# Attention scores in PSUM tiles of two banks, in a hybrid decoder layer on one Trainium2 core

## The chip, the core and the metric

The program runs on one NeuronCore of a Trainium2 chip. TensorE (PE in the profile) multiplies, VectorE (DVE), ScalarE (ACT) and GpSimd (POOL) do the rest, and SyncE (SP) issues the transfers. TensorE writes into PSUM, which has eight banks here; one bank holds 512 float32 numbers in each of 128 partitions. The metric is the device time of one execution in microseconds (us). The time before is 1449.49 us, the median of three runs that lie between 1445.99 and 1454.82 us.

## What is computed

One decoder layer on a sequence of 1024 tokens: a modulation from a conditioning vector, one input projection, two groups of attention heads side by side, an output projection, and a gated feed-forward layer with a short convolution. Only the attention matters here:

```
group A (8 heads, 96 numbers in q and k): scores of all keys up to the query, softmax, times v
group B (8 heads, 64 numbers in q and k): the same, over three dilated windows that are combined
                                          by their softmax denominators
mix = concat(A, B) @ w_o
```

The kernel does group B as one dense attention too: a mask that is added to the scores holds minus the logarithm of how many of the three windows take a key (and a large number where none does), so both groups run through the same code with two different masks. Every product is made of three: an operand is split into a rounded part `hi` and a rest `lo`, and hi x hi, hi x lo and lo x hi are added up in PSUM.

## The kernel before

**The attention stage.** Eight couples of heads are worked through, four of group B (called dilated here) and four of group A (called MLA), in the order 0, 4, 1, 5, 2, 6, 3, 7, so that a dilated couple and an MLA couple alternate (L690 to L709). For each couple there are two halves of the queries, `hf` 0 and 1, of four blocks of 128 queries each. Block `qi` sees `w = 128 * (qi + 1)` keys, so the rows of the first half are 128, 256, 384 and 512 wide and those of the second 640, 768, 896 and 1024.

**Scores** (`scores`, L624). A row of scores needs three matmuls per 512 columns at most. A row of the first half goes into one PSUM bank, tile `s`; a row of the second half is cut into two equal parts of 320, 384, 448 and 512 columns, each with a bank of its own. VectorE then adds the mask, writes the sum to SBUF (`pt`) and keeps the smallest number of each row, in one instruction per bank (L642, shown as CUSTOM_DVE, with a short DVE_READ_ACCUMULATOR2 behind it); the second part of a wide row starts from the smallest number of the first part (its operand `st`). ScalarE takes the exponential with its row sum (L646), GpSimd turns the sum into its inverse (L647) and scales the row (L648). The buffers of `pt` are two for each block number, one per head (`P_BUFS`).

**The two heads of a couple on TensorE.** The heads of a dilated couple have 64 numbers each and lie in partitions 0 to 63 and 64 to 127 of the same tiles `q2` and `k2`; their matmuls use 64 of the 128 rows of TensorE (64\*128 in the rows of the trace). The heads of an MLA couple have 96 numbers and tiles of their own (96\*128). For a dilated couple the source puts the matmuls of both heads next to each other (`together`).

**Weighted values** (`weighted_values`, L662). The scaled rows are turned by TensorE, four blocks of 128 x 128 into one bank (tile `x`, L671); ScalarE writes the rounded part `pT_hi` (L677), VectorE the rest `pT_lo` (L678), which reads the same bank and sets it free; two matmuls per tile, one with `hi` and one with `lo`, add to the output in tile `o` (L682). A half of a couple has 6 such `x` tiles for `hf` 0 and 14 for `hf` 1. The half that is worked through is the one before (`pending`), so that weighted values of one half stand beside the scores of the next. The turned q and k of the next couple (`transposed`, L529 to L533) use banks of the same pool `x`: L529 on TensorE, L531 on ScalarE, L532 on VectorE.

**PSUM in this stage** (L614): 3 banks for `x`, 2 for `o`, 3 for `s`.

**What sets the order.** The instructions are recorded in the order of the source, and a scheduler then puts them in order for each engine by a simulated timeline: an instruction can move past others of its engine where its operands and buffers are free earlier. The couple's matmuls that stand next to each other in the source need not do so in the program. Each engine then works through its own list in that order.

Of the kernel before, what the change touches and what calls it, by code (L numbers as in the profile page):

```python
# [8 lines left out]
F32 = mybir.dt.float32  # L9
# [3 lines left out]
AF = mybir.ActivationFunctionType  # L13
ALU = mybir.AluOpType
# [4 lines left out]
P = 128  # L19
S = 1024  # L20
# [11 lines left out]
P_BUFS = 2  # L32
# [9 lines left out]
def hybrid_layer(ctx, tc, x, c, positions, w_ada, b_ada, g_mix_norm, w_in, g_q_lat, w_q_b, g_kv_lat, w_kv_b,  # L42
# [3 lines left out]
    V, G, A, T = nc.vector, nc.gpsimd, nc.scalar, nc.tensor  # L46
    x, c, out = x[0], c, out[0]
# [10 lines left out]
    def psum_phase(**tags):  # L58
        psum.close()
        pools.clear()  # L60
        for tag, n in tags.items():
            pools[tag] = psum.enter_context(
                tc.tile_pool(name="ps_" + tag, bufs=n, space=PSUM, reuse_waits="tile"))
# [3 lines left out]
    def bank(tag="bank"):  # L67
        return pools[tag].tile([P, 512], F32, tag=tag, name=tag)

    def wide():  # L70
        return pools["wide"].tile([P, 1024], F32, tag="wide", name="wide")
# [41 lines left out]
    negone = cp.tile([P, 1], F32, name="negone")  # L113
# [150 lines left out]
    def proj_weights(c0, n):  # L264
        raw = raw_tile(KD, n)
        nc.sync.dma_start(raw, w_in[:, c0:c0 + n].rearrange("(k p) n -> p k n", p=P))
        return split_weights(raw, KD, n)
# [5 lines left out]
    def proj_mm(w, t, n):  # L273
        ps = bank("p")
        for k in range(KD):
            proj_step(ps, w, t, n, k)
        return ps
# [59 lines left out]
    ap = phA.enter_context(tc.tile_pool(name="phAw", bufs=1, reuse_waits="tile"))  # L337
# [103 lines left out]
    w = proj_weights(C_KV, 288)  # L441
    for t in range(NT):
# [3 lines left out]
        ps = proj_mm(w, t, 288)  # L446
# [9 lines left out]
        b = ap.tile([P, 1, ROPE], F32, tag="peb", name="peb", bufs=2)  # L456
# [7 lines left out]
    for u in range(2):  # L464
# [6 lines left out]
        w = proj_weights(C_VD + u * 256, 256)  # L471
        for t in range(NT):
            ps = proj_mm(w, t, 256)
            o = ap.tile([P, 256], F32, tag="vo", name="vo", bufs=6)
# [16 lines left out]
    for hf in range(2):  # L491
        cs = slice(hf * 512, hf * 512 + 512)
        for src, hi, lo, n, g0 in ((q_lat, ql_hi, ql_lo, 4, G0_QL), (kv_lat, kl_hi, kl_lo, 2, G0_KV)):
            for f in range(n):
                ps = bank("x")
# [57 lines left out]
    for u in range(2):  # L553
        raw = raw_tile(4, 384)
        nc.sync.dma_start(raw, w_q_b[:, u * 384:(u + 1) * 384].rearrange("(k p) n -> p k n", p=P))
        w = split_weights(raw, 4, 384)
        for t in range(NT):
            ts_ = slice(t * P, (t + 1) * P)
            ps = bank("p")
# [12 lines left out]
            o = mp.tile(b3, F32, tag="ro", name="rom", bufs=4)  # L572
# [6 lines left out]
            b = mp.tile(bp, F32, tag="rb", name="rbm", bufs=3)  # L579
# [4 lines left out]
    for u in range(2):  # L584
        raw = raw_tile(2, 512)
        nc.sync.dma_start(raw, w_kv_b[:, u * 512:(u + 1) * 512].rearrange("(k p) n -> p k n", p=P))
        w = split_weights(raw, 2, 512)
        for t in range(NT):
            ts_ = slice(t * P, (t + 1) * P)
            ps = bank("p")  # L590
            for k in range(2):
# [11 lines left out]
            o = mp.tile([P, 4, MW], F32, tag="ro", name="rok", bufs=4)  # L603
            V.tensor_tensor(o[:, :, 0:NOPE], p3[:, :, 0:NOPE], r[:, :, None].to_broadcast(b3), op=ALU.mult)
            G.tensor_scalar(o[:, :, NOPE:MW], k_pe[:, t:t + 1, :].to_broadcast([P, 4, ROPE]), 1.0, 0.0,
                            op0=ALU.mult, op1=ALU.add)
# [4 lines left out]
    more_weight_buffers(None, 0)  # L611


    psum_phase(x=3, o=2, s=3)  # L614
    phM = ExitStack()
    mxp = phM.enter_context(tc.tile_pool(name="mixbuf", bufs=1, reuse_waits="tile"))
    mix = mxp.tile([P, 8, S], F32, name="mix")
# [2 lines left out]
    ap = phB.enter_context(tc.tile_pool(name="phB", bufs=1, reuse_waits="tile"))  # L620
    GROUPS = ([((0, 0),), ((1, 1), (3, 3)), ((2, 2),)],
              [((0, 0),), ((1, 0),), ((2, 0),), ((3, 0),), ((4, 0),), ((5, 1), (7, 3)), ((6, 2),)])

    def scores(hf, heads, mask, together):  # L624
        prs = [[] for _ in heads]
        for group in ([heads] if together else [[h] for h in heads]):
            for i in range(4):
                qi = 4 * hf + i
                w = P * (qi + 1)
                qs_ = slice(qi * P, (qi + 1) * P)  # L630
                cuts = [(0, w)] if w <= 512 else [(0, w // 2), (w // 2, w)]
                pts = [ap.tile([P, w], F32, tag=f"pt{qi}", name=f"pt{qi}", bufs=P_BUFS) for _ in group]
                sts = [ap.tile([P, 4], F32, tag="st", name="st", bufs=16) for _ in group]
                for n, (a, b) in enumerate(cuts):
                    pss = [bank("s") for _ in group]
                    for m in range(len(group[0])):
                        for ps, terms in zip(pss, group):
                            q_, k_ = terms[m]
                            T.matmul(ps[:, 0:b - a], lhsT=q_[:, qs_], rhs=k_[:, a:b], start=(m == 0),  # L639
                                     stop=(m == len(terms) - 1))  # L640
                    for ps, pt, st in zip(pss, pts, sts):
                        V.tensor_tensor_reduce(pt[:, a:b], ps[:, 0:b - a], mask[:, S - w + a:S - w + b], 1.0,  # L642
                                               3.0e38 if n == 0 else st[:, n - 1:n], ALU.add, ALU.min, st[:, n:n + 1])
                m = len(cuts) - 1
                for terms, pt, st in zip(group, pts, sts):
                    A.activation(pt, pt, AF.Exp, bias=st[:, m:m + 1], scale=-1.0, accum_out=st[:, 2:3])  # L646
                    G.tensor_tensor(st[:, 3:4], st[:, 2:3], negone, op=ALU.pow)  # L647
                    G.tensor_scalar(pt, pt, st[:, 3:4], 1.0, op0=ALU.mult, op1=ALU.mult)  # L648
                    prs[[h is terms for h in heads].index(True)].append(pt)
        return prs  # L650

    evac = [0]
# [40 lines left out]
    for n, pr in enumerate(ORDER):  # L693
        mask = masks[:, 1 if pr < 4 else 0, :]
# [89 lines left out]
    for hf in range(2):  # L784
# [4 lines left out]
        for cch in range(4):  # L789
# [6 lines left out]
            w = split_weights(raw, KD, 256)  # L796
            pss = []
            for i in range(4):
                ps = bank()
# [234 lines left out]
    for hf in range(2):  # L1034
        pss = {(i, u): bank("d") for i in range(4) for u in range(2)}
# [13 lines left out]
        for ff in range(NFF):  # L1049
            w, m = down_parts(ff), m_parts(ff, hf)  # L1050
# [6 lines left out]
        for i in range(4):  # L1057
            t = 4 * hf + i
            for u in range(2):
# [3 lines left out]
                o = fp.tile([P, 512], F32, tag="s", name="o", bufs=4)  # L1063
# [43 lines left out]
```

## Time and profile before

| | |
|---|---|
| median of three runs | 1449.49 us |
| the profiled execution: device time | 1452.97 us |
| its span, first to last instruction | 1451.0 us |
| granted TensorE clock, mean | 0.979 |
| TensorE busy | 1376.4 us, 95% |
| VectorE busy | 972.6 us, 67% |
| GpSimd busy | 795.5 us, 55% |
| ScalarE busy | 727.4 us, 50% |
| the attention stage, in the span | 352 to 652 us |

The profiled execution is one run; its device time is the span and 1.97 us around it, and it lies 3.5 us above the median. In the stage's 300 us TensorE is busy for 285.2 us, VectorE for 247.5, ScalarE for 237.7. A matmul's busy time includes the end of its way through the array, though, so two that follow each other overlap; what a matmul costs is read from start to start. "Idle before" in a row is the time in which the engine had nothing under way, with what ended it. Columns are times from the span's start.

### The profile page before, as it was taken

What the parts mean: (1) busy time and instruction counts of PE and PEld (TensorE: products, weight loads), DVE (VectorE), ACT (ScalarE), POOL (GpSimd) and SP (SyncE); (2) the same over time, 40 slices, a digit from 0 to 9 for tenths busy, and PEclk for the clock granted to TensorE, in tenths of its full rate; (3) what the DMA queues carried; (4) which work ended last, traced back from release to release, by engine and by line L of the source; (5) the groups of instructions that cost most, each with busy time, mean ns of one, the idle gap of its engine ahead of it and who ended that gap; (6) DMA issues with size and microseconds to landing.
All of it is one profiled execution on the core that took longest, in us unless ns stands there. A gap on an engine that the chain in (4) does not pass through costs nothing.

```text
span 1451.0 us, 22006 instructions
## 1 busy us (share of the span) xinstructions
PE 1376.4 (95%) x7837; PEld 1178.1 (81%) x7837; DVE 972.6 (67%) x1834; ACT 727.4 (50%) x1409; POOL 795.5 (55%) x780
## 2 busy tenths in 40 slices
PE   5889999998999998989989799999999999999998
PEld 3789999996778786779978688888888887888887
DVE  3667888687878888875655767777777765226213
ACT  3524322376778887864444644455455454322320
POOL 3355656367766667534624275656655554555552
PEclk9999999999999999999999899999999999999999
DMA  9643354546121114003535122222222238445431
GB/s 320 197 149 120 125 184 158 112 152 212 31 59 45 59 45 116 2 17 124 195 114 177 59 97 76 88 88 71 75 87 88 87 113 307 162 144 191 160 113 58
DMA packets 140197, 173.31 MB, mean 119 GB/s; under 512 B 7986, under 2 KB 118968, under 8 KB 139960
## 3 DMA queue, kind: packets, MB, share of 16 engines
q1 hardware_dynamic: 140088, 171.92, 36.5%
q8 instruction: 61, 1.00, 0.3%
q14 instruction: 48, 0.39, 0.1%
HBM read 135.19 MB, written 36.70 MB: 118 GB/s over the span
## 4 chain that ended last, share of the span: by engine, by line
PE 63%; DVE 5%; DMA 4%; POOL 3%; ACT 3%; issue 3%; SPq 0%; DVEq 0%; POOLq 0%; ACTq 0%
PE d L1045 16%; PE X L877 16%; PE Z L877 8%; PE Y L877 5%; PE o L682 5%; PE s L639 4%; PE x L671 4%; DMA raw<-in_w_o_dram 2%; POOL w_lo L98 2%; PE p L103 1%; DVE pt L642 1%; PE p L104 1%; PE p L105 1%; ACT pt L646 1%; PE bank L105 1%
## 5 line engine op out<-in xcount | busy, mean ns | idle before, releaser
L1045 PE MATMUL d<-wd,m 128*128 128x512 f32 x1056 | 240.0, 389 | 3.2 <-ACT m L1028 3.0
L1045 PEld LDWEIGHTS d<-wd,m 128*128 128x128 f32 x1056 | 198.0, 188 | 45.1 <-ACT m L1028 3.4
L830 POOL TENSOR_TENSOR wa<-sum,wa 128x512 fp32r<-128x512 f32 x80 | 135.1, 1692 | 119.0 <-ACT wa L829 118.1
L1021 POOL TENSOR_TENSOR wd<-raw,wd 128x512 fp32r<-128x512 f32 x88 | 132.5, 1528 | 112.0 <-ACT wd L1018 96.3
L877 PE MATMUL X<-T,wa 128*128 128x512 f32 x720 | 172.2, 392 | 8.6 <-ACT wa L829 8.6
L103 PE MATMUL p<-w_hi,h_hi 128*128 128x256 f32 (+1 forms) x576 | 165.2, 288 | 3.2 <-ACT xn L362 3.2
L877 PEld LDWEIGHTS X<-T,wa 128*128 128x128 f32 x720 | 136.3, 190 | 37.6 <-ACT wa L829 9.0
L98 POOL TENSOR_TENSOR w_lo<-raw,w_hi 128x512 fp32r<-128x512 f32 (+3 forms) x74 | 109.8, 1514 | 97.8 <-ACT w_hi L92 97.8
L104 PE MATMUL p<-w_lo,h_hi 128*128 128x256 f32 (+1 forms) x576 | 163.4, 285 | 0.0
L105 PE MATMUL p<-w_hi,h_lo 128*128 128x256 f32 (+1 forms) x576 | 161.1, 286 | 1.0 <-DVE h_lo L262 1.0
L830 POOL TENSOR_TENSOR wa<-raw,wa 128x512 fp32r<-128x512 f32 x68 | 100.8, 1488 | 85.9 <-ACT wa L829 85.4
L1029 DVE TENSOR_TENSOR m<-m_raw,m 128x512 fp32r<-128x512 f32 x44 | 54.4, 1242 | 123.9 <-ACT m L1028 123.9
L1018 ACT ACTIVATE wd<-raw 128x1024 fp32r<-128x1024 f32 x44 | 46.6, 1059 | 142.6 <-PE d L1045 117.5
L647 POOL TENSOR_TENSOR st<-st,negone 128x1 f32<-128x1 f32 x128 | 69.9, 553 | 83.7 <-ACT pt L646 72.7
L103 PEld LDWEIGHTS p<-w_hi,h_hi 128*128 128x128 f32 x576 | 111.1, 193 | 3.6 <-ACT xn L362 3.4
L104 PEld LDWEIGHTS p<-w_lo,h_hi 128*128 128x128 f32 x576 | 111.4, 193 | 0.1
L678 DVE TENSOR_TENSOR pT_lo<-x,pT_hi 128x512 fp32r<-128x512 f32 (+1 forms) x160 | 98.0, 633 | 19.6 <-ACT pT_hi L677 18.5
L105 PEld LDWEIGHTS p<-w_hi,h_lo 128*128 128x128 f32 x576 | 109.0, 192 | 1.6 <-DVE h_lo L262 1.6
L677 ACT ACTIVATE pT_hi<-x 128x512 fp32r<-128x512 f32 (+1 forms) x160 | 86.0, 553 | 46.0 <-PE x L671 39.5
L929 DVE SCALAR_TENSOR_TENSOR y<-c,ccols,y 128x1023 f32<-128x1023 f32 x44 | 60.5, 1376 | 62.3 <-ACT y L928 61.5
L646 ACT ACTIVATE pt<-pt,st 128x256 f32<-128x256 f32 (+7 forms) x128 | 98.5, 772 | 6.3 <-DVE st L642 6.1
L648 POOL TENSOR_SCALAR pt<-pt,st 128x256 f32<-128x256 f32 (+7 forms) x128 | 97.6, 768 | 6.6
(265 smaller groups left out, 3385.4 us busy)
## 6 DMA issues: line engine op xcount, KB each, us to landing
raw<-in_w_up_dram SPq DMA_DIRECT2D x22, 1024.0 KB, 9.2
raw<-in_w_down_dram SPq DMA_DIRECT2D x22, 1024.0 KB, 5.1
raw<-in_w_ada_dram SPq DMA_DIRECT2D x16, 1024.0 KB, 8.2
m_s<-y SPq DMA_DIRECT2D x22, 512.0 KB, 2.6
m_raw<-m_s SPq DMA_DIRECT2D x44, 256.0 KB, 2.8
ada<-in_w_ada_dram SPq DMA_DIRECT2D x8, 1024.0 KB, 5.3
raw<-in_w_in_dram SPq DMA_DIRECT2D x8, 1024.0 KB
raw<-in_w_o_dram SPq DMA_DIRECT2D x16, 512.0 KB, 3.5
```

The lines of the kernel that those rows point to most:

```text
L98: G.tensor_tensor(lo[:, i:i + 2, :], raw[:, i:i + 2, :], hi[:, i:i + 2, :].bitcast(F32), op=ALU.subtract)
L103: T.matmul(ps, lhsT=a[0], rhs=b[0], start=first, stop=False)
L104: T.matmul(ps, lhsT=a[0], rhs=b[1], start=False, stop=False)
L105: T.matmul(ps, lhsT=a[1], rhs=b[0], start=False, stop=last)
L646: A.activation(pt, pt, AF.Exp, bias=st[:, m:m + 1], scale=-1.0, accum_out=st[:, 2:3])
L648: G.tensor_scalar(pt, pt, st[:, 3:4], 1.0, op0=ALU.mult, op1=ALU.mult)
L677: A.activation(hi[:, 0:c0], px[:, 0:c0], AF.Copy)
L678: V.tensor_tensor(lo[:, 0:c0], px[:, 0:c0], hi[:, 0:c0].bitcast(F32), op=ALU.subtract)
L830: eng.tensor_tensor(lo, src, hi.bitcast(F32), op=ALU.subtract)
L877: T.matmul(four(ps), lhsT=wt[:, a, kt, :], rhs=b, start=(first and kt == 0 and m == 0), stop=(kt == 3 and m == 2), skip_group_check=True)
L1021: G.tensor_tensor(lo[:, cs], raw[:, cs], hi[:, cs].bitcast(F32), op=ALU.subtract)
L1045: T.matmul(pss[i, u], lhsT=m[a][:, ts_], rhs=w[b][:, cs], start=(ff == 0 and k == 0), stop=(ff == NFF - 1 and k == 2))
```

## The change

The scores move to PSUM tiles of two banks, tile `wide`, of which there are two; the pool of `x` gets two banks where it had three; `o` keeps two.

- Rows of the first half: both heads of a couple share one `wide` tile, a bank each, and both heads of a block are worked through before the next block, for MLA couples too.
- Rows of the second half: a head's whole row is in one `wide` tile, its two parts in the two banks. The mask's addition and the smallest number are then one instruction with the whole row, in place of two.
- The source puts the matmuls of a dilated couple next to each other (`steps.sort()`), those of an MLA couple head after head.

The number of matmuls, exponentials, scalings and transfers stays the same. Lines behind the function stand two higher: L639 becomes L641, L642 becomes L647, L671 becomes L673, L677 and L678 become L679 and L680, L682 becomes L684.

```diff
-    psum_phase(x=3, o=2, s=3)
+    psum_phase(x=2, o=2, wide=2)
...
-    def scores(hf, heads, mask, together):
-        prs = [[] for _ in heads]
-        for group in ([heads] if together else [[h] for h in heads]):
-            for i in range(4):
-                qi = 4 * hf + i
-                w = P * (qi + 1)
-                qs_ = slice(qi * P, (qi + 1) * P)
-                cuts = [(0, w)] if w <= 512 else [(0, w // 2), (w // 2, w)]
-                pts = [ap.tile([P, w], F32, tag=f"pt{qi}", name=f"pt{qi}", bufs=P_BUFS) for _ in group]
-                sts = [ap.tile([P, 4], F32, tag="st", name="st", bufs=16) for _ in group]
-                for n, (a, b) in enumerate(cuts):
-                    pss = [bank("s") for _ in group]
-                    for m in range(len(group[0])):
-                        for ps, terms in zip(pss, group):
-                            q_, k_ = terms[m]
-                            T.matmul(ps[:, 0:b - a], lhsT=q_[:, qs_], rhs=k_[:, a:b], start=(m == 0),
-                                     stop=(m == len(terms) - 1))
-                    for ps, pt, st in zip(pss, pts, sts):
-                        V.tensor_tensor_reduce(pt[:, a:b], ps[:, 0:b - a], mask[:, S - w + a:S - w + b], 1.0,
-                                               3.0e38 if n == 0 else st[:, n - 1:n], ALU.add, ALU.min, st[:, n:n + 1])
...
+    def scores(hf, heads, mask, overlap):
+        prs = [[], []]
+        for i in range(4):
+            qi = 4 * hf + i
+            w = P * (qi + 1)
+            qs_ = slice(qi * P, (qi + 1) * P)
+            if hf == 0:
+                both = wide().rearrange("p (h n) -> p h n", n=512)
+                views = [both[:, h:h + 1, 0:w] for h in range(2)]
+            else:
+                views = [wide().rearrange("p (c n) -> p c n", n=512)[:, :, 0:w // 2] for _ in range(2)]
+            nc_, n = (1, w) if hf == 0 else (2, w // 2)
+            steps = [(c_, m, h) for h in range(2) for c_ in range(nc_) for m in range(3)]
+            if overlap:
+                steps.sort()
+            for c_, m, h in steps:
+                q_, k_ = heads[h][m]
+                T.matmul(views[h][:, c_, :], lhsT=q_[:, qs_], rhs=k_[:, c_ * n:(c_ + 1) * n], start=(m == 0),
+                         stop=(m == 2))
+            for h in range(2):
+                pt = ap.tile([P, w], F32, tag=f"pt{qi}", name=f"pt{qi}", bufs=P_BUFS)
+                st = ap.tile([P, 4], F32, tag="st", name="st", bufs=16)
+                parts_ = [a.rearrange("p (c n) -> p c n", n=n) for a in (pt, mask[:, S - w:S])]
+                V.tensor_tensor_reduce(parts_[0], views[h], parts_[1], 1.0, 3.0e38, ALU.add, ALU.min, st[:, 0:1])
...
```

The scheduler's order moves with it. In the rows below the names are tile<-operands with their buffer numbers, then the output's size; "x2" is two equal instructions in a row. Three places on TensorE follow.

**The second dilated couple, first half, the 384 columns of both heads.** Before, each head has a bank (`s_5655`, `s_5656`):

```order
L639 MATMUL s_5655<-k2_5510,q2_5494 128x384
L639 MATMUL s_5655<-k2_5511,q2_5494 128x384
L639 MATMUL s_5655<-k2_5510,q2_5495 128x384
L682 MATMUL o_5527<-pT_lo_5545,vs_5127 128x512
L671 MATMUL x_5576<-ident_72,pt2_5152 128x128
L671 MATMUL x_5576<-ident_72,pt3_5162 128x128
L639 MATMUL s_5656<-k2_5510,q2_5494 128x384
L639 MATMUL s_5656<-k2_5511,q2_5494 128x384
L639 MATMUL s_5656<-k2_5510,q2_5495 128x384
```

Now they share `wide_5609`:

```order
L673 MATMUL x_5510<-ident_72,pt2_5157 128x128
L673 MATMUL x_5510<-ident_72,pt3_5176 128x128 x2
L641 MATMUL wide_5609<-k2_5470,q2_5454 128x384 x2
L641 MATMUL wide_5609<-k2_5471,q2_5454 128x384 x2
L641 MATMUL wide_5609<-k2_5470,q2_5455 128x384 x2
L684 MATMUL o_5487<-pT_hi_5504,vs_5107 128x512
```

The second head's three matmuls stood behind three instructions of other kinds; now each stands right behind the first head's equal one, in one run of six.

**The same couple, second half, the first row of each head (640 wide, two parts of 320).** Before, part by part:

```order
L671 MATMUL x_5693<-ident_72,pt7_5419 128x128
L639 MATMUL s_5857<-k2_5510,q2_5494 128x320
L639 MATMUL s_5857<-k2_5511,q2_5494 128x320
L639 MATMUL s_5857<-k2_5510,q2_5495 128x320
L682 MATMUL o_5526<-pT_lo_5580,vs_5127 128x256
```

Now head by head, both parts of the first head (`wide_5809`) and then both of the second (`wide_5810`):

```order
L684 MATMUL o_5487<-pT_hi_5548,vs_5107 128x256
L641 MATMUL wide_5809<-k2_5470,q2_5454 128x320
L641 MATMUL wide_5809<-k2_5471,q2_5454 128x320
L641 MATMUL wide_5809<-k2_5470,q2_5455 128x320
L641 MATMUL wide_5809<-k2_5470,q2_5454 128x320
L641 MATMUL wide_5809<-k2_5471,q2_5454 128x320
L641 MATMUL wide_5809<-k2_5470,q2_5455 128x320
L641 MATMUL wide_5810<-k2_5470,q2_5454 128x320
L641 MATMUL wide_5810<-k2_5471,q2_5454 128x320
```

The runs became longer, but the two heads of a wide row stand one behind the other, not side by side. Over all four dilated couples the runs of such matmuls, with no other kind between, go from 70 to 41: before 40 runs of three, 18 of six (in these, too, the second head's three behind the first head's three) and 12 of other lengths; now 28 of six, 7 of twelve, and three each of four and eight.

**Weighted values of the couple before, beside it.** Before, three banks turn:

```order
L671 MATMUL x_5715<-ident_72,pt4_5374 128x128
L671 MATMUL x_5715<-ident_72,pt5_5389 128x128
L671 MATMUL x_5715<-ident_72,pt6_5404 128x128
L671 MATMUL x_5715<-ident_72,pt7_5419 128x128
L671 MATMUL x_5726<-ident_72,pt4_5434 128x128
L671 MATMUL x_5726<-ident_72,pt5_5449 128x128
L671 MATMUL x_5726<-ident_72,pt6_5464 128x128
L671 MATMUL x_5726<-ident_72,pt7_5479 128x128
L682 MATMUL o_5691<-pT_hi_5698,vs_5127 128x512
L682 MATMUL o_5691<-pT_lo_5699,vs_5127 128x512
L682 MATMUL o_5691<-pT_hi_5720,vs_5127 128x512
```

Now two:

```order
L673 MATMUL x_5671<-ident_72,pt4_5364 128x128
L673 MATMUL x_5671<-ident_72,pt5_5390 128x128
L673 MATMUL x_5671<-ident_72,pt6_5416 128x128
L673 MATMUL x_5671<-ident_72,pt7_5442 128x128
L684 MATMUL o_5648<-pT_hi_5665,vs_5107 128x512
L684 MATMUL o_5647<-pT_hi_5676,vs_5107 128x512
L684 MATMUL o_5648<-pT_lo_5666,vs_5107 128x512
L673 MATMUL x_5682<-ident_72,pt4_5370 128x128
L673 MATMUL x_5682<-ident_72,pt5_5396 128x128
L673 MATMUL x_5682<-ident_72,pt6_5422 128x128
L673 MATMUL x_5682<-ident_72,pt7_5448 128x128
L684 MATMUL o_5647<-pT_lo_5677,vs_5107 128x512
```

Before, two tiles are turned in a row while the results of the two before them are not yet used (`pT_hi_5698` is the first of them). Now the four turns of a tile stand right behind the matmul that uses the `lo` part of the tile two before, and there is one tile between.

## Rows read from the trace of the kernel before

**Rows 1.** Window: us; PE, PEld, DVE, ACT, POOL busy; clock, DMA share, GB/s.

```profile
406.00:549.00 143.00, 140.72 (x857) 112.37 (x857) 121.13 (x310) 117.52 (x254) 89.75 (x135) 1.00 0.18 52
```

**Rows 2.** Waits of TensorE, 352 to 652 us: total us, times, longest.

```profile
PE x L529 <- ACT vs L658: 3.7, 1, 3.7
PE o L682 <- DVE pT_lo L678: 3.4, 1, 3.4
PE s L639 <- DVE st L642: 3.0, 4, 1.3
```

**Rows 3.** Timeline of TensorE, dilated scores: start, us, instruction, count.

```profile
414.21 0.97 PE L639 MATMUL s<-k,q 64*128 64x512 f32 x3
415.11 0.45 PE L682 MATMUL o<-pT_hi,vs 128*128 128x384 f32 x1
415.49 0.96 PE L639 MATMUL s<-k,q 64*128 64x512 f32 x3
...
500.26 0.38 PE L671 MATMUL x<-ident,pt 128*128 128x128 f32 x2
500.57 0.78 PE L639 MATMUL s<-k,q 64*128 64x384 f32 x3
501.28 0.50 PE L682 MATMUL o<-pT_hi,vs 128*128 128x512 f32 x1
...
503.93 0.80 PE L639 MATMUL s<-k,q 64*128 64x384 f32 x6
504.66 0.44 PE L682 MATMUL o<-pT_lo,vs 128*128 128x384 f32 x1
```

**Rows 4.** The same: the first, the third and the last run of dilated scores.

```profile
317.81 0.33 PE L639 MATMUL s<-k,q 64*128 64x128 f32 x2
...
326.79 0.38 PE L639 MATMUL s<-k,q 64*128 64x256 f32 x1
...
592.17 1.31 PE L639 MATMUL s<-k,q 64*128 64x512 f32 x6
```

**Rows 5.** Groups of VectorE by form, 352 to 652 us: count, busy, mean ns, idle before.

```profile
L642 DVE CUSTOM_DVE_ANT_0 pt<-s,masks 128x512 f32<-128x512 f32 x32 | 21.7, 684 | 1.1 <-POOL st L647 0.8
L642 DVE DVE_READ_ACCUMULATOR2_ANT st<- 128x1 f32 x192 | 15.6, 81 | 0.0
L642 DVE CUSTOM_DVE_ANT_0 pt<-s,masks,st 128x512 f32<-128x512 f32 x16 | 11.9, 745 | 1.3 <-PE s L639 0.9
L642 DVE CUSTOM_DVE_ANT_0 pt<-s,masks 128x128 f32<-128x128 f32 x16 | 4.4, 282 | 0.0
```

**Rows 6.** Timelines of TensorE, ScalarE and VectorE, 457 to 464 us, weighted values.

```profile
457.33 0.60 PE L671 MATMUL x<-ident,pt 128*128 128x128 f32 x4
...
459.01 0.60 PE L671 MATMUL x<-ident,pt 128*128 128x128 f32 x4
...
459.68 1.04 PE L671 MATMUL x<-ident,pt 128*128 128x128 f32 x8
460.57 0.73 PE L682 MATMUL o<-pT_hi,vs 128*128 128x512 f32 x2
461.14 0.40 PE L682 MATMUL o<-pT_lo,vs 128*128 128x512 f32 x1
461.37 0.39 PE L682 MATMUL o<-pT_hi,vs 128*128 128x512 f32 x1
...
462.29 0.60 PE L671 MATMUL x<-ident,pt 128*128 128x128 f32 x4
...
462.92 0.60 ACT L677 ACTIVATE pT_hi<-x 128x512 fp32r<-128x512 f32 x1 [0.98 <-PE x L671]
...
460.74 0.69 DVE L678 TENSOR_TENSOR pT_lo<-x,pT_hi 128x512 fp32r<-128x512 f32 x1
```

**Rows 7.** Timelines: the stage's first `x` tile on TensorE, the last `pT_lo` on VectorE.

```profile
352.44 1.91 PE L529 MATMUL x<-ident,ql_t 128*96 128x128 f32 x8 [3.69 <-ACT vs L658]
...
647.55 1.42 DVE L678 TENSOR_TENSOR pT_lo<-x,pT_hi 128x512 fp32r<-128x512 f32 x3 [0.45 <-ACT pT_hi L677]
```

More of the change, by code (lines that the diff above doesn't have):

```diff
@@ L622, in hybrid_layer @@
               [((0, 0),), ((1, 0),), ((2, 0),), ((3, 0),), ((4, 0),), ((5, 1), (7, 3)), ((6, 2),)])
-    def scores(hf, heads, mask, together):
-        prs = [[] for _ in heads]
-        for group in ([heads] if together else [[h] for h in heads]):
-            for i in range(4):
-                qi = 4 * hf + i
-                w = P * (qi + 1)
-                qs_ = slice(qi * P, (qi + 1) * P)
-                cuts = [(0, w)] if w <= 512 else [(0, w // 2), (w // 2, w)]
-                pts = [ap.tile([P, w], F32, tag=f"pt{qi}", name=f"pt{qi}", bufs=P_BUFS) for _ in group]
-                sts = [ap.tile([P, 4], F32, tag="st", name="st", bufs=16) for _ in group]
-                for n, (a, b) in enumerate(cuts):
-                    pss = [bank("s") for _ in group]
-                    for m in range(len(group[0])):
-                        for ps, terms in zip(pss, group):
-                            q_, k_ = terms[m]
-                            T.matmul(ps[:, 0:b - a], lhsT=q_[:, qs_], rhs=k_[:, a:b], start=(m == 0),
-                                     stop=(m == len(terms) - 1))
-                    for ps, pt, st in zip(pss, pts, sts):
-                        V.tensor_tensor_reduce(pt[:, a:b], ps[:, 0:b - a], mask[:, S - w + a:S - w + b], 1.0,
-                                               3.0e38 if n == 0 else st[:, n - 1:n], ALU.add, ALU.min, st[:, n:n + 1])
[L644 to L649, printed above, removed]
@@ new lines, in scores @@
+    def scores(hf, heads, mask, overlap):
[22 more added lines that the diff above has]
+                V.tensor_tensor_reduce(parts_[0], views[h], parts_[1], 1.0, 3.0e38, ALU.add, ALU.min, st[:, 0:1])
+                A.activation(pt, pt, AF.Exp, bias=st[:, 0:1], scale=-1.0, accum_out=st[:, 2:3])
+                G.tensor_tensor(st[:, 3:4], st[:, 2:3], negone, op=ALU.pow)
+                G.tensor_scalar(pt, pt, st[:, 3:4], 1.0, op0=ALU.mult, op1=ALU.mult)
+                prs[h].append(pt)
```

## The prediction, as it was made before the changed kernel ran

> **What bounds the kernel now.** I read the busy time by stretch first, then TensorE's waits, then the timelines of the three engines in the attention stage. The stage takes 300 of the span's 1451 us. In its even middle TensorE is busy for 140.7 of 143 us, VectorE for 121.1 and ScalarE for 117.5, so 85% and 82% [rows 1]. The reader should set beside this how little TensorE waits: the three largest sums of waits in the whole stage come to 10.1 us, and none of them is for a bank of `x`; for a bank of `s` (the reduction's `st`) it waits 3.0 us [rows 2]. So TensorE's own list of instructions sets the pace, and the other two follow it at some distance. A microsecond taken off that list is worth about one; a microsecond off VectorE is worth little as long as TensorE doesn't wait for it.
>
> The second thing to see is what a visit of TensorE to dilated scores costs, read from start to start [rows 3]. Three matmuls of one head at 384 columns hold the engine from 500.57 to 501.28, 0.71 us; six of both heads hold it from 503.93 to 504.66, 0.73 us. The second head is free if it stands beside the first. Three at 512 columns take 0.90 us, of which the columns are 0.69, since a full matmul of 512 columns takes 0.23 (461.14 to 461.37, [rows 6]); 0.21 us is the price of the visit. Entering costs more: one 384-column matmul ahead of a visit takes 0.38 us (415.11 to 415.49, [rows 3]) where its columns are worth 0.17, and two turns take 0.31 (500.26 to 500.57) where eight take 0.89, or 0.22 for two [rows 3, 6]. So a visit not made saves another 0.09 to 0.21 us.
>
> The third is the life of an `x` tile, from its first turn to the end of its `lo`. There are 204 in the stage, 160 of weighted values and 44 of turned q and k, the first at 352.44, the last set free at 648.97 [rows 7]. Their lives add up to 636.7 us, 3.1 us each. Three banks offer 890 us in those 296.5 us, two offer 593.
>
> **TensorE's list.** The 70 runs of dilated scores of before last 56.0 us, each from its first start to the next instruction's start, idle left out; the first, the third and the last of them are in [rows 4]. Of the 41 runs after, those of the first half have both heads side by side: per couple 0.38 and 0.56 us for the runs of four and eight (0.21 plus the columns of one head), 0.73 for 384 and 0.91 for 512; with the first couple's two runs of twelve (0.73 and 1.41) that is 9.9 us. In the second half a head's six stand alone: 0.71 + 3 x 0.17 = 1.23 us at 384, and by the same rate 1.40 at 448 and 1.59 at 512, each twice per couple, 8.4 us. The 320-column rows stand as a run of twelve, head behind head: 1.06 us if the hardware puts them side by side, 1.94 if not. Four couples make 38.0 to 41.5 us. The total is 47.9 to 51.4, a saving of 4.6 to 8.1 us; 29 entries fewer save 2.6 to 6.1 more. I take **-10.5 us**, in the middle of 7.2 and 14.2.
>
> Whether a run that is written head behind head goes side by side is shown by before: its runs of six are written so, and the one at 503.93 costs 0.73 us and not the 0.71 + 3 x 0.17 = 1.22 of six in a row [rows 3]. The Trainium skill (TensorE: Matmul & The Clock Gate, Part 3) says that matmuls start and end strictly in program order, and that only weight loads are pulled ahead. By that rule such a run gains nothing, the 320-column rows cost 1.94 us, and the saving would be nearer 8.5 us; this row speaks against it.
>
> The nine matmuls of the first couple that stood among the projections, 317.81 to 327.1 [rows 4], now stand behind the last projection. They took 1.2 us; at 352 us TensorE idles 3.7 us anyway for the values' split [rows 7], which hides them. From 0 to +1.2 us; I take **+0.5**.
>
> **VectorE.** A reduction of 128 columns takes 282 ns, one of 512 takes 684: 1.05 ns a column and 148 ns for the instruction [rows 5]. A 1024-wide row costs 684 + 745 + 2 x 81 = 1591 ns today, and as one instruction about 148 + 1072 + 81 = 1301. At 0.29 us for each of 64 wide rows VectorE gets 18.6 us back. No row shows one instruction over two banks; if the second bank costs another 148 ns, it gets 9.1 us back. On the path this is worth **0**: TensorE's list covers it. The most it can give are the 6.4 us that TensorE waits for `st` and `pT_lo` in the stage [rows 2]. If the cover goes, the longer instruction (1.22 us where the longest was 0.75) is what a `pT_lo` stands behind in VectorE's queue, and behind that `pT_lo` the turn that wants its bank. The MLA rows of the first half, the exponentials, GpSimd's two instructions and SP's transfers only change places.
>
> **The banks of `x`.** This is the unknown. Lower end: nothing. The shortest life is 0.60 turning, 0.60 on ScalarE and 0.69 on VectorE, 1.9 us, as the rows of 462.29, 462.92 and 460.74 have them [rows 6]; two banks then start a tile every 0.95 us, and from the tile at 457.33 to the one at 462.29 there are four steps of 1.24 us today. Upper end: each tile of before held back until the tile two ahead of it is free, everything behind it shifted and nothing filled in, adds up to 79 us over the 204 tiles. Between them stands the count of lives: 636.7 us in two banks need 318.4 us, 21.9 more than the 296.5; if VectorE's 18.6 us come off the lives, 309.1, or 12.5 more. Against a full price speaks that the 44 tiles of q and k live 4.1 us each because nobody wants their banks, 2 us longer than they need; for it, that a bank stands empty until TensorE's list comes to the next turn. I take **+15 us**, between the two counts, since the lives of today are the nearest thing that the trace shows.
>
> **Sum.** -10.5 + 0.5 + 0 + 15 = +5 us. On the profiled execution's 1452.97 us that is 1458; that execution lies 3.5 us above the median of 1449.49, and against the median the forecast is **1454.5 us**.
>
> **Rivals.**
> *The banks of `x` set the pace (slower).* The place is the stretch in which both `wide` tiles are full of 320-column rows, whose `pt` buffers come free only when the couple before has turned its first blocks. TensorE then has turns and `o` matmuls alone, and each turn stands right behind the `lo` matmul of the tile two before. From there on TensorE waits for VectorE once per tile. It decides when a mean life and the time until the bank is used again exceed twice the 1.47 us of a tile (300 / 204), 2.9 us; today's 3.1 is already above. If lives stay and a bank is empty for 0.1 us between, the stage needs (636.7 + 20) / 2 = 328 us, +32, less the 10 saved: +22, **1472 us**; with 0.25 us empty, 1487. Against it: lives today are long partly because a third bank lets tiles be turned early. The Trainium skill (Perfetto Trace Analysis, Identifying Performance Opportunities) reads a gap that repeats on the engine that should be saturated as a sign that PSUM may be too small for the next tile; before shows no such gap [rows 2].
> *Two banks are enough (faster).* Lives fall below 2.7 us, TensorE's steps of 1.24 us [rows 6] and more hide them, and the shorter reductions give the 6.4 us of waits back: -10.5 - 5 = -15, **1434.5 us**. For it: the shortest life is far under the limit. Against it: ScalarE and VectorE are over 80% busy, so few tiles find both free.
> *The couples don't go together.* Most wide rows stay apart in the list, as the order shows, and if even the first half's runs don't pair, the saving is the 29 entries, 2.6 to 6.1 us: +11, **1460.5 us**. The pairing rows speak against it.
>
> **Chances.** One per cent, 14.5 us, is about what a measurement of this kernel can tell from no change. Forecast 0.42, within 1%; banks set the pace 0.32, slower; two banks enough 0.18, faster; couples not together 0.08, within 1%. So faster 0.18, within 1% 0.50, slower 0.32. The range goes from the faster rival's 1434 to between the two prices of the slower one, 1480, with a little under 2 in 10 outside; the forecast's own is 1443 to 1464.
>
> **What would show it.** In the changed profile the dilated matmuls should have fewer starts behind another kind, with pairs some ns apart in the first half; the reductions of wide rows near 0.82 to 1.22 us, 64 fewer, VectorE 9 to 19 us less busy. A wait of the turns or of the `o` matmuls for `pT_lo` that adds up to 10 us or more in the stage is the price of two banks; over 30 us is the slower rival, under 5 the faster one. The forecast is wrong if the time moves outside the stage, or if it moves with reductions that cost more than two of the old ones.

## The result, and the profile after

| | before | after |
|---|---|---|
| median (four runs each) | 1452.15 us | 1526.03 us |
| range | 1445.99 to 1457.47 | 1521.84 to 1527.84 |
| ratio to before, 95% interval | | 1.0512 [1.0477, 1.0546] |
| span of the profiled execution | 1451.0 us | 1526.1 us |
| granted TensorE clock, mean over the span | 0.979 | 0.958 |
| the attention stage, first `x` tile to last `pT_lo` | 296.5 us | 369.5 us |

The change makes the kernel 74 us slower; the forecast was 1454.5 us with a range up to 1480. The attention stage alone accounts for 73 of the 75 us by which the profiled spans differ, so the rest of the program plays almost no part.

I read the stage as a whole first: before's stretch and after's. Columns as in [rows 1].

```profile
352.44:648.97 296.53, 284.76 (x1702) 227.44 (x1702) 245.78 (x621) 235.74 (x506) 190.05 (x277) 0.98 0.17 49
```

```profile
355.90:725.40 369.50, 327.26 (x1701) 252.72 (x1699) 238.94 (x488) 241.10 (x507) 186.53 (x275) 0.90 0.13 38
431.00:520.00 89.00, 79.23 (x433) 61.27 (x432) 59.55 (x124) 60.49 (x129) 45.91 (x68) 0.94 0.15 42
...
367.10:391.00 23.90, 23.90 (x79) 18.39 (x78) 12.55 (x28) 12.66 (x27) 17.64 (x27) 0.50 0.24 67
...
469.40:472.90 3.50, 3.50 (x17) 3.28 (x18) 2.05 (x4) 2.27 (x4) 3.34 (x4) 0.51 0.06 19
```

Two things are to be seen. TensorE has nothing under way for 369.50 - 327.26 = 42.2 us, where it was 296.53 - 284.76 = 11.8; that is 30 us. And its granted clock over the stage is 0.90 where it was 0.98. The clock has two levels, 2.4 and 1.2 GHz, so about 20% of the stage ran at the lower one. In matmul work that is at most 0.10 x 369.5 = 37 us lost, against 6 before: up to 31 us more. (At most, since TensorE waits in such a stretch too.) These two make 61 of the 73 us. The second row of after is the answer to [rows 1]: two couples take 89 us, where before had 71.5, and no engine is over 90% busy. I read this as a stage that no engine bounds any more: they wait for each other.

Next I read who waits. TensorE's and its weight loads' waits, then ScalarE's and VectorE's, in after's stage: total us, times, longest.

```profile
PE wide L641 <- ACT khi L531: 8.5, 5, 2.4
PE wide L641 <- DVE st L647: 7.4, 14, 4.5
PE wide L641 <- ACT k L531: 6.5, 3, 2.2
PE o L684 <- ACT pT_hi L679: 5.1, 23, 0.9
...
PE o L684 <- DVE pT_lo L680: 3.9, 6, 2.8
...
PEld o L684 <- ACT pT_hi L679: 27.5, 72, 1.1
...
PEld o L684 <- DVE pT_lo L680: 10.8, 22, 3.1
...
ACT pT_hi L679 <- PE x L673: 99.9, 85, 5.0
...
DVE pt L647 <- PE x L673: 51.2, 48, 2.6
DVE pT_lo L680 <- ACT pT_hi L679: 29.3, 39, 1.2
```

The same waits of the weight loads, and for the turns, in the stage of before:

```profile
PEld o L682 <- ACT pT_hi L677: 6.8, 20, 0.9
...
PEld o L682 <- DVE pT_lo L678: 5.8, 8, 3.7
...
ACT pT_hi L677 <- PE x L671: 39.5, 53, 5.4
...
DVE pt L642 <- PE x L671: 5.6, 9, 1.1
```

ScalarE waits for a turn for 99.9 us instead of 39.5. VectorE's reductions (L647) wait 51.2 us instead of 5.6 until a turn has read the old `pt` and so set its buffer free. While such a reduction waits, all that stands behind it on VectorE waits too, and `pT_lo`, which sets a bank of `x` free, is among that. TensorE's own answer to [rows 2] is spread over many small waits: 15.0 us (8.5 + 6.5) for ScalarE's split of the next k, 7.4 for a `wide` tile, 9.0 (5.1 + 3.9) for `pT_hi` and `pT_lo`. The loads of its weights, which run beside the matmul before, wait 38.3 us (27.5 + 10.8) for the same two tiles, where before has 12.6.

One turn of this wheel, 457 to 470 us, on TensorE, VectorE and ScalarE: start, us, instruction, count, idle before.

```profile
458.38 1.48 PE L641 MATMUL wide<-k,q 64*128 64x448 f32 x6
459.79 0.38 PE L684 MATMUL o<-pT_hi,vs 128*128 128x256 f32 x1
460.10 1.66 PE L641 MATMUL wide<-k,q 64*128 64x512 f32 x6
...
462.14 0.40 PE L673 MATMUL x<-ident,pt 128*128 128x128 f32 x2
...
469.32 0.67 PE L641 MATMUL wide<-khi,qhi 96*128 96x128 f32 x2 [2.27 <-ACT khi L531]
...
458.97 1.02 DVE L680 TENSOR_TENSOR pT_lo<-x,pT_hi 128x512 fp32r<-128x512 f32 x2
462.58 1.09 DVE L647 CUSTOM_DVE_ANT_0 pt<-wide,masks 128x896 f32<-128x896 f32 x1 [2.59 <-PE x L673]
...
462.64 0.38 ACT L679 ACTIVATE pT_hi<-x 128x256 fp32r<-128x256 f32 x1 [2.37 <-PE x L673]
...
468.59 0.68 ACT L531 ACTIVATE khi<-x,kgc 96x512 fp32r<-96x512 f32 x1
```

VectorE has finished both tiles by 459.99 (458.97 + 1.02). The next turn comes at 462.14, 2.15 us later, because a six of scores (460.10, 1.66 us) and some `o` matmuls stand ahead of it in TensorE's list. VectorE idles 2.59 us, ScalarE 2.37. When the turn has come, both have a queue: reductions, exponentials, then the split of the next k at 468.59. For that TensorE waits 2.27 us, and right behind this gap its clock stands at 1.2 GHz (0.51 in the row 469.40:472.90). A third bank could have held one more turned tile for ScalarE and VectorE to work on during the scores.

The reductions, the answer to [rows 5], by form, 356 to 726 us:

```profile
L647 DVE CUSTOM_DVE_ANT_0 pt<-wide,masks 128x1024 f32<-128x1024 f32 x16 | 19.4, 1215 | 4.1 <-PE wide L641 4.1
L647 DVE CUSTOM_DVE_ANT_0 pt<-wide,masks 128x896 f32<-128x896 f32 x16 | 17.4, 1089 | 16.1 <-PE x L673 15.0 <-PE wide L641 1.1
...
L647 DVE CUSTOM_DVE_ANT_0 pt<-wide,masks 128x640 f32<-128x640 f32 x16 | 13.2, 823 | 14.4 <-PE x L673 14.4
```

A second bank costs the instruction nothing that shows: 1215 ns for 1024 columns and 823 for 640, where 148 ns and 1.05 a column [rows 5] give 1223 and 820. All reductions together with their short companions take 93.4 + 10.6 = 104.0 us in the stage where they took 67.0 + 40.9 + 15.6 = 123.5.

### The profile page after: what moved, and what is told of

Its sections match the earlier page's. It is cut to its first block, busy times and chain, and to the rows that moved or that the text cites. A ratio compares the mean times of both kernels' runs of the same rounds, so it can differ in the third digit from the quotient of the medians.

```text
span 1526.1 us, 21916 instructions
## 1 busy us (share of the span) xinstructions
PE 1417.8 (93%) x7837; PEld 1204.6 (79%) x7837; DVE 969.2 (64%) x1706; ACT 731.7 (48%) x1409; POOL 792.4 (52%) x780
## 4 chain that ended last, share of the span: by engine, by line
PE 62%; ACT 5%; DVE 4%; DMA 4%; issue 4%; POOL 3%; SPq 0%; DVEq 0%; ACTq 0%; POOLq 0%
PE d L1047 16%; PE X L879 15%; PE Z L879 8%; PE wide L641 6%; PE Y L879 4%; PE o L684 4%; PE x L673 3%; DMA raw<-in_w_o_dram 2%; ACT pT_hi L679 1%; POOL w_lo L98 1%; ACT pt L648 1%; PE x L529 1%; PE p L103 1%; PE p L104 1%; PE p L105 1%
## 5 line engine op out<-in xcount | busy, mean ns | idle before, releaser
L679 ACT ACTIVATE pT_hi<-x 128x512 fp32r<-128x512 f32 (+1 forms) x160 | 87.8, 553 | 104.3 <-PE x L673 99.9
L647 DVE CUSTOM_DVE_ANT_0 pt<-wide,masks 128x256 f32<-128x256 f32 (+7 forms) x128 | 93.4, 754 | 67.3 <-PE x L673 51.2
L680 DVE TENSOR_TENSOR pT_lo<-x,pT_hi 128x512 fp32r<-128x512 f32 (+1 forms) x160 | 98.6, 634 | 29.8 <-ACT pT_hi L679 29.3
```

Source lines behind the costliest of these rows:

```text
L679: A.activation(hi[:, 0:c0], px[:, 0:c0], AF.Copy)
L680: V.tensor_tensor(lo[:, 0:c0], px[:, 0:c0], hi[:, 0:c0].bitcast(F32), op=ALU.subtract)
```

## The experiments

Three causes were open at first. **T1**: the third bank of `x`. **T2**: the score tiles of two banks (fewer units, held longer, one long instruction). **T3**: MLA couples worked through block by block. Times are medians; ratios are to the kernel before, run on the same chip beside each group, with their 95% intervals, and they are what is compared across groups. Each edit also moves the scheduler's order, so a run shows an edit together with the order that comes with it.

### One bank of x less, and the bank given to the scores

```diff
-    psum_phase(x=3, o=2, s=3)
+    psum_phase(x=2, o=2, s=3)      # e2; e1: s=4; e7: s=2
```

> The kernel before with x=2, o=2, s=3, one bank left unused: the third bank of x is taken away alone. T1: 1500 to 1535 us. T2 and T3: 1450 to 1480 us. Against e1 it also tells what a fourth score bank is worth: nothing by T1, 5 to 20 us by T2, since more score banks in flight would then be the good that is short.

> The kernel before with the change's split of the banks only: x=2, o=2, s=4 (four score tiles of one bank each, where the change has two of two banks). Theory T1, the third bank of x is what costs the 74 us: 1500 to 1530 us, and the turns wait for pT_lo or VectorE for the turns much as after (the reductions' wait for turns near 50 us, before 5.6). Theory T2, the size of the score tiles costs it (two units that are held for as long as a row waits): 1450 to 1475 us, that wait under 15 us. Theory T3, the blocks' order in MLA couples costs it: 1450 to 1470 us as by T2.

> The kernel before with x=2, o=2, s=2, two banks unused. With two banks of x, four score banks took 1529 us and three took 1500. If a score bank more lets more reductions stand ahead of pT_lo in VectorE's list, where they wait for the turns that want the bank: 1475 to 1498 us, reductions waiting for turns under 20 us (28.7 with three, 38.6 with four). If the fourth bank was bad for another reason: 1500 to 1540 us, because scores then also miss banks.

| x=2, o=2 with | us | ratio | reductions wait for turns |
|---|---|---|---|
| s=3 (e2) | 1500.24 | 1.0332 [1.0307, 1.0356] | 28.7 us |
| s=4 (e1) | 1528.58 | 1.0508 [1.0455, 1.0562] | 38.6 us |
| s=2 (e7) | 1498.96 | 1.0329 [1.0274, 1.0385] | 5.1 us |

The bank alone costs 48 us, on the old code. The change's whole split of banks, still with single score banks, costs as much as the change (e1 1528.58, after 1526.03). So T1 holds for the greater part, and the size is reached without tiles of two banks (T2) and without the new order of blocks (T3). The other 26 us of it come in e1 with the fourth score bank, though, and that was foreseen by neither theory. The reductions' wait for turns, expected near 50 us in e1, is 38.6. In the stage the difference between e2 and e1 is in idle time (343.60 - 316.89 = 26.7 us against 371.90 - 338.41 = 33.5) and above all in the clock, 0.93 against 0.88:

```profile
352.60:696.20 343.60, 316.89 (x1703) 238.16 (x1702) 248.43 (x616) 239.11 (x507) 188.05 (x275) 0.93 0.14 41
```

```profile
353.70:725.60 371.90, 338.41 (x1700) 254.34 (x1699) 249.36 (x616) 241.74 (x507) 187.37 (x275) 0.88 0.13 38
```

e7 was a test of the idea that reductions waiting for turns are what hurts. That wait nearly goes (5.1 us), and the time stays; the reductions now wait for scores:

```profile
DVE pt L642 <- PE s L639: 33.6, 38, 2.3
DVE pt L642 <- PE x L671: 5.1, 12, 0.8
```

So 1475 to 1498 was missed by a hair, and the wait under 20 us came without the gain that was tied to it. What follows is that two banks of `x` cost their 48 us with two score banks as with three.

### Block by block, with the old banks

```diff
-        for group in ([heads] if together else [[h] for h in heads]):
+        for group in [heads]:
...
-                    for m in range(len(group[0])):
-                        for ps, terms in zip(pss, group):
...
+                    steps = [(m, h) for h in range(2) for m in range(3)]
+                    if together:
+                        steps.sort()
```

> The kernel before, with its banks, but MLA couples worked through block by block with both heads, as the change does it (three matmuls of one head, then three of the other). T3, this order costs: 1480 to 1525 us, with VectorE's reductions waiting for turns 30 us or more. T1 and T2: within 10 us of 1452.

1460.06 us, 1.0065 [1.004, 1.009]: 8 us slower by the medians, inside what T1 and T2 expected, and the reductions wait 2.9 us for turns. With three banks of `x`, T3 is at most a small part; with two no run has it alone.

### Two reductions per wide row

```diff
-                V.tensor_tensor_reduce(parts_[0], views[h], parts_[1], 1.0, 3.0e38, ALU.add, ALU.min, st[:, 0:1])
+                for c_ in range(nc_):
+                    V.tensor_tensor_reduce(pt[:, c_ * n:(c_ + 1) * n], views[h][:, c_, :], ...,
+                                           3.0e38 if c_ == 0 else st[:, 0:1], ALU.add, ALU.min, st[:, c_:c_ + 1])
...
```

> The kernel after, but a wide row's addition and minimum are two instructions again, one per bank, on the same tile of two banks. If the longer reduction in VectorE's queue is what blocks pT_lo and so the turns (a part of T2): 1470 to 1505 us. If the tiles themselves or the bank of x cost it (the other part of T2, or T1): 1520 to 1550 us, since VectorE gets 18.6 us more of work and nothing else changes.

1515.98 us, 1.0442 [1.0416, 1.0468], which lies below after's interval: 10 us faster, between the two expectations, although VectorE has 20 us more to do. Its reductions wait for turns in shorter pieces:

```profile
DVE pt L647 <- PE x L675: 29.1, 46, 1.4
```

The longest wait is 1.4 us where after had 2.6, and the sum 29.1 where it had 51.2. By form, all of it falls on the first reduction of a row; the second ones wait for no turn. So a shorter reduction still waits for its whole `pt` buffer, and why it waits less is not shown. That one long instruction held VectorE's queue is one reading; the scheduler's new order is another.

### The third bank given back, and its control

```diff
-    psum_phase(x=2, o=2, wide=2)
+    psum_phase(x=3, o=1, wide=2)      # e5; e9 keeps x=2, o=2
...
-        pos = [bank("o") for _ in prs]
...
-        for grp in GROUPS[hf]:
-            for odd, pr in enumerate(prs):
+        for odd, pr in enumerate(prs):
+            po = bank("o")
+            for grp in GROUPS[hf]:
...
```

> The kernel after with its third bank of x given back, taken from o: x=3, o=1, wide=2, and since one bank of o cannot hold both heads, the weighted values of a half go head after head. T1, the third bank of x is what the change lost: 1450 to 1485 us, TensorE idle in the attention stage under 20 us (42 after, 12 before) and 15 to 50 us of it at the lower clock (76 after, 13 before). T2, tiles of two banks cost something of their own: 1500 us or more. One bank of o may cost up to 16 waits of 1 to 2 us for its output to be copied, which is inside the first range.

> The kernel after with its own banks (x=2, o=2, wide=2), but the weighted values of a half go head after head, as in the run with x=3, o=1 (1463.8 us). It tells whether the bank or the order gave the 62 us back. The bank: 1505 to 1535 us. The order: under 1480 us.

e5: 1463.76 us, 1.0066 [1.004, 1.0092]. e9: 1512.35 us, 1.0431 [1.0411, 1.0451]. The order of heads gives 0.8% back, and then the bank 3.7%, or 53 us: on the new code the third bank is worth about what it is on the old. With it, what is left of the change, the bank of `o` that was given up included, costs under 1%. e5's stage idles 307.10 - 289.05 = 18.1 us, inside what T1 expected, and its longest stretch at the lower clock is the second row:

```profile
351.10:658.20 307.10, 289.05 (x1699) 239.15 (x1698) 236.81 (x489) 236.97 (x507) 189.82 (x275) 0.93 0.16 46
361.10:391.80 30.70, 30.39 (x96) 23.52 (x97) 15.51 (x32) 15.43 (x34) 17.36 (x25) 0.50 0.15 43
```

What the bank changes on TensorE is seen in the waits of its weight loads for `pT_hi` and `pT_lo`, first e9, then e5 (which has none for `pT_hi`):

```profile
PEld o L684 <- DVE pT_lo L680: 32.1, 67, 3.2
PEld o L684 <- ACT pT_hi L679: 15.1, 35, 1.2
```

```profile
PEld o L684 <- DVE pT_lo L680: 2.7, 8, 0.5
```

With two banks the `o` matmuls stand so close behind their turn that both splits are waited for, 47.2 us in sum; with three it is 2.7.

### A third buffer for two of the eight `pt` blocks

```diff
-                pt = ap.tile([P, w], F32, tag=f"pt{qi}", name=f"pt{qi}", bufs=P_BUFS)
+                pt = ap.tile([P, w], F32, tag=f"pt{qi}", name=f"pt{qi}", bufs=3 if qi in (0, 4) else P_BUFS)
```

> The kernel after with a third buffer in SBUF for the first row of each half (blocks 0 and 4, pt0 and pt4); there is no room for more. If reductions that wait for their pt buffer in front of pT_lo are what closes the circle on two banks: 1490 to 1515 us, with the reductions' wait for turns under 35 us (51.2 after). If the banks of x alone set the pace, whoever waits: 1518 to 1532 us.

1510.34 us, 1.0376 [1.033, 1.0423]: 16 us faster than after by the medians, 20 by the ratios, with everything in PSUM as it was. The wait in question fell:

```profile
DVE pT_lo L680 <- ACT pT_hi L679: 42.1, 70, 1.5
DVE pt L647 <- PE x L673: 27.4, 31, 2.6
```

27.4 us, where after has 51.2, as expected; VectorE's wait for `pT_hi` rose from 29.3 to 42.1 meanwhile. So reductions that stand in VectorE's list ahead of their buffer are a part of the loss in the new code. They are not the whole of it: e9 has 14.0 us of this wait and takes 1512, e7 5.1 us and 1499.

### More banks of x

```diff
-    psum_phase(x=3, o=2, s=3)
+    psum_phase(x=4, o=2, s=2)      # e6, on the kernel before
```

> The kernel before with a bank moved the other way: x=4, o=2, s=2. If the pace goes with the banks of x (T1): 1435 to 1452 us, the turns' part of VectorE's waits under 5.6 us. If three banks were enough and the scores now miss theirs: 1452 to 1480 us with TensorE's score matmuls waiting for the reductions 10 us or more (3.0 before).

1476.79 us, 1.0147 [1.011, 1.0185]. A bank moved the other way is no gain either: VectorE's reductions now wait for scores, not the score matmuls for reductions as expected (5.4 us):

```profile
DVE pt L642 <- PE s L639: 32.7, 51, 2.2
```

The bank must come from elsewhere. With heads one after the other (as in e5) `o` needs one bank, and on the kernel before the free one can go to `x` (e10) or to the scores (e11). e12 is e10 with the third `pt` buffers of e8.

```diff
-    psum_phase(x=3, o=2, s=3)
+    psum_phase(x=4, o=1, s=3)      # e10 and e12; e11: x=3, o=1, s=4
```

> The kernel before with heads one after the other in the weighted values and the bank of o that this sets free given to x: x=4, o=1, s=3. If before is already at TensorE's list with three banks of x: 1445 to 1458 us. If more banks of x still help: 1430 to 1445 us. If one bank of o makes TensorE wait for its copy, 16 times 1 to 2 us: 1460 to 1480 us.

> The same with the bank given to the scores: x=3, o=1, s=4. With two banks of x a fourth score bank cost 28 us (1500 to 1529). If a fourth score bank is bad in itself: 1465 to 1490 us. If it is bad only where x has two banks: 1440 to 1462 us, the pace of before.

> The version with x=4, o=1, s=3 and heads one after the other (1440.8 us), with a third buffer in SBUF for the first row of each half as in the run that gained 16 us on the kernel after. If reductions that wait for these buffers still hold back VectorE's queue: 1425 to 1437 us. If that mattered only with two banks of x, because TensorE's list sets the pace here: 1436 to 1446 us.

e10: 1440.75 us, 0.9944 [0.9923, 0.9965]. e11: 1460.30 us, 1.0066 [1.0049, 1.0084]. e12: **1434.50 us, 0.9882 [0.9856, 0.9908]**, faster than both kernels of this case. A bank is worth 18 us more with the turns than with the scores. e11 lies in the range for a fourth score bank that is bad only where `x` has two, e10 in the one for more banks that still help, and e12 in the one for reductions that still hold back VectorE's queue. e12's stage:

```profile
348.80:632.50 283.70, 274.53 (x1699) 223.46 (x1700) 244.45 (x622) 230.99 (x507) 187.53 (x278) 0.98 0.17 51
380.00:460.00 80.00, 79.31 (x506) 66.08 (x505) 71.46 (x188) 67.50 (x151) 56.45 (x87) 1.00 0.17 47
```

TensorE idles 9.2 us in the stage, and in its even part 0.7 of 80: here the pace is again that of its list.

### Two reductions, with three banks of x

> The kernel with tiles of two banks and the third bank of x back (x=3, o=1, heads one after the other, 1463.8 us), with two reductions per wide row as in the run that was 10 us faster than the kernel after. If the one long reduction costs in itself, by what stands behind it in VectorE's queue: 1445 to 1458 us. If it costs only where x has two banks: 1460 to 1475 us, since VectorE gets 18.6 us of work more and TensorE's list hides most of it.

The edit is that of "Two reductions per wide row", on e5. 1457.57 us, 1.0038 [1.0009, 1.0067], against e5's 1.0066 [1.004, 1.0092]. The median lies in the first range, but the intervals overlap. The long reduction is not shown to cost anything once the third bank is there, nor to gain anything.

## Why the prediction was wrong

**The step that failed: the banks of `x`, +15 us.** Their price is 48 us alone (e2), and 53 with the new scores (e9 to e5). The +15 counted lives alone: 636.7 us in two banks instead of three. That a bank also stands empty until TensorE's list comes to the next turn was named and put at nothing in the sum, and at 0.1 to 0.25 us in the slower rival. After's 204 tiles live 553.6 us (553.6 / 204 = 2.71 us each, from the first turn to the end of the `lo`), less than the 636.7 assumed. But a bank is used once in 2 x 369.5 / 204 = 3.62 us, so it stands empty for 0.91 us of them. Life and empty time together are 3.62 us, over the 2.9 at which the slower rival said that the banks decide. Before's own trace held the empty time: three banks, 3 x 296.5 / 204 = 4.36 us per use, less lives of 3.12 (the 636.7 us of [rows 7]'s stretch), is 1.24 us. That it is a freed bank's wait for its place in TensorE's list is seen at 459.99 to 462.14 above; how much of it is that everywhere is not shown.

The empty time is no constant, though: 0.69 us in e2, 0.91 in after, 1.30 with four banks (4 x 288.0 / 204 - 4.35, e10), 0.40 in e6. Kept whole with the lives of before, 1.24 us would have given a stage of 445 us, 148 more. What bracketed the price were two other counts of the prediction: the lives alone, 21.9 us, from below, and the replay in TensorE's order with nothing filled in, 79 us, from above. It took its value under both.

**What the sum left out: the clock.** [rows 1] showed 1.00, and the prediction had no term for it. Up to 31 of the 73 us are TensorE's lower level (1.2 GHz). After's longest stretch of it is the row 367.10:391.00 above, at 0.50. What TensorE did just before:

```profile
365.61 0.64 PE L529 MATMUL x<-ident,ql_t 128*96 128x128 f32 x4 [1.28 <-DVE klo L532]
366.90 0.95 PE L529 MATMUL x<-ident,ql_t 128*96 128x128 f32 x4 [0.64 <-DVE klo L532]
```

Two waits of 1.28 and 0.64 us, both for VectorE, and then 24 us at 1.2 GHz. The Trainium skill (TensorE: Matmul & The Clock Gate, A second HAM failure mode: psum-queue depth-cycling) describes a kernel that cycles through PSUM banks, idles briefly between groups of matmuls and loses throughput to a clock that falls and rises; this trace agrees, with 0.90 where before has 0.98. How much of the 31 us is the clock's own, and how much TensorE would have waited anyway, no run separates. Nor is all of it the third bank's: e5, which has that bank, has an even longer stretch at 0.50 at the same place (30.70 us, from within a wait of 1.10 us on), and 0.93 over its stage. From e9 (350.2 us at 0.92) to e5 (307.1 at 0.93) the clock can account for at most 0.08 x 350.2 - 0.07 x 307.1 = 6.5 of the 43 us.

**TensorE's list, -10.5 us.** Its mechanism held in part. The runs are 41 as said, but take 61.2 us instead of 47.9 to 51.4, and so more than before's 56.0. 8.6 us of that are the lower clock, by an estimate from the same runs at the upper level (after's other couples, and e5's for the first), 52.6 us. So at the upper level they save 3.4 us, less than the 4.6 to 8.1 forecast. What the 29 entries fewer saved no run separates; e5 leaves room for it: TensorE is busy 4.3 us more there than before, though by the same count its lower clock can have cost up to 15 more. First-half runs pair, 0.72 and 0.89 us (431.94 to 432.66, 434.53 to 435.42), as forecast. The 320-column run does not:

```profile
431.94 0.80 PE L641 MATMUL wide<-k,q 64*128 64x384 f32 x6
432.66 0.50 PE L684 MATMUL o<-pT_hi,vs 128*128 128x512 f32 x1
...
434.53 0.96 PE L641 MATMUL wide<-k,q 64*128 64x512 f32 x6
435.42 0.56 PE L684 MATMUL o<-pT_hi,vs 128*128 128x384 f32 x2
...
437.56 2.18 PE L641 MATMUL wide<-k,q 64*128 64x320 f32 x12
439.68 0.39 PE L684 MATMUL o<-pT_lo,vs 128*128 128x256 f32 x1
```

It takes 2.12 us (437.56 to 439.68), over both of the prediction's prices, 1.06 and 1.94. Before's run at 503.93 has three of one head behind three of the other, and its matmuls start in pairs, 8 to 10 ns apart; here six stand behind six, and the seventh starts 1.03 us behind the first. For that run the Trainium skill's rule of strict order (TensorE: Matmul & The Clock Gate, Part 3) holds; for runs of three behind three the row that the prediction quoted still speaks against it.

**VectorE, 0.** The forecast size of what it gets back was right: 18.6 us, measured 123.5 - 104.0 = 19.5. The sentence behind it, that a longer instruction is what a `pT_lo` stands behind if the cover goes, fits what came: with two banks of `x` the merged instruction costs 10 us (e4), though by which wait is not shown.

**The rivals.** The slower one had the right cause and sign, and was priced at 1472 to 1487. Its mark failed: in the rows that the prediction read, TensorE's waits for `pT_lo` are 3.9 us, which it had given to the faster rival. They are 10.8 on the weight loads, but 5.8 there before, and the larger wait stood one step earlier, for `pT_hi`, 5.1 and 27.5. TensorE's largest waits of all, 15.0 us for the next k and 7.4 for a `wide` tile, no rival had priced. Its place was too narrow: in the stretch that has turns and `o` matmuls alone, 439.68 to 449.94, TensorE idles 1.1 us of 10.3, in the 19.4 us behind it 3.0:

```profile
439.68:449.94 10.26, 9.16 (x50) 6.30 (x49) 5.98 (x11) 6.05 (x13) 2.52 (x5) 1.00 0.01 2
449.94:469.32 19.38, 16.38 (x82) 11.74 (x82) 13.14 (x25) 13.31 (x27) 10.97 (x15) 1.00 0.00 1
```

**What stays open.** About 12 us or more of the 73 are in TensorE's busy time at the upper clock (73 less 30 idle and at most 31 clock). A matmul's busy time includes the end of its way, so a weight load that waits behind it can hide there; the 25.7 us (38.3 - 12.6) more of such waits are the likely place, which is not shown. A bank less also gives TensorE another list, and no run has the old list with two banks, so what the bank costs by itself and what by its list is not separated. And why a fourth score bank costs 28 us with two banks of `x` is shown only as far as its trace: more reductions waiting for turns, more idle time, a lower clock.

## What to carry to other kernels

Before taking a buffer away, bracket its price from the trace. Here the lives of the tiles, counted against the buffers that are left, gave 21.9 us, and a replay of the old order, in which each tile waits for the buffer that it would now get and nothing is filled in, gave 79; 48 to 53 were measured. Neither is a bound in general, since lives and order change too. Where the bound engine has almost no waits, ask what its first ones could set off: a gap of a microsecond or two was followed by the lower clock here (1.28 + 0.64 us, and 2.27). In this kernel a bank was worth most with `x`, which feeds two other engines; `o` could spare one, and the turns took 9 us out of the kernel with it (e10), 18 with two more `pt` buffers (e12).

## What the runs showed of the hardware that was not expected

- One reduction over two PSUM banks costs no more per column than over one: 1215 ns for 1024 columns in two banks, 685 for 512 in one, so 1.04 ns a column, about what [rows 5] give for one bank.
- TensorE's clock fell to 1.2 GHz behind two gaps that added up to 1.92 us (between 364.3 and 366.9) and stayed there for 24 us in which TensorE was busy throughout (23.90 of 23.90 us). In e5 it fell within a wait of 1.10 us, and stayed there for 30.7 us with TensorE busy for 30.39.
- Matmuls of two heads on different rows of the array go side by side where three of one stand behind three of the other (0.73 us for six of 384 columns, [rows 3]), and not where six stand behind six (2.12 us for twelve of 320).
